# Third head pair's mask order and the start of the recurrence in a one-layer hybrid encoder kernel

## The chip, the cores and the metric

The kernel runs on one core of one Trainium2 chip, in float32. The time is device microseconds (us) of one launch; the number that is compared is the median of several executions. TensorE is called PE below, VectorE DVE, ScalarE ACT, GpSimd POOL, and SyncE, which here only issues transfers, SP.

## The reference

One layer of a two-branch block over 528 frames (16 meta tokens and 512 real ones), width 2048, and a final RMSNorm. Cut to what matters:

```python
hn = rmsnorm(h_res, norm_in_g);  P = hn @ w_in            # 2048 -> 8320 columns
Pr, Pc = P[..., :RW_COLS], P[..., RW_COLS:]
Pr = Pr + (prev(Pr) - Pr) * mu_shift                      # r, k, v, g, two low-rank inputs
# branch A, 16 heads of 64: S_t = S_{t-1} diag(w_t) - (S_{t-1} kk_t)(kk_t*a_t)^T + v_t k_t^T
#                           y_t = S_t r_t, then a norm per head, a bonus and a gate
# branch B: y_b = B * conv3(C * h) * silu(g_c)
h_res = h_res + concat(y_a, y_b) @ w_out
out = rmsnorm(h_res, norm_f_g)[:, 16:]
```

## The kernel before

**Projection.** Every matrix product in full precision is three matmuls of split operands: weights and activations are each written as a rounded high part and a low remainder (`xh`, `xl` for the activations; `hi`, `lo` of a slot `w` for the weights), and hi·xh, hi·xl and lo·xh are added up in PSUM (`steps`, matmul on L328). A column block of 128 outputs is called by what it gives: `lora`, `k`, `r`, `v`, `g` for branch A, one of each per head pair, and `C`, `h`, `B`, `gc` for branch B. The 65 blocks come one after another in the order of `plan`; this stream of matmuls is the generator `flow`. A block of 528 or 514 columns takes two PSUM banks (`ps_k_0`, `ps_k_1`) and 96 matmuls, a block of 512 takes one bank and 48. The weights come by transfers of 512 KB (`wr`, L142, three buffers), two quarters to a transfer; each quarter is cast to its high part on ACT (L134) and its low part is made on DVE or POOL (L135), in six slots `w`. A slot comes free when PE has done with the quarter in it.

**Branch A** needs a chain of small work per head pair (eight pairs). `prepare(i)` makes the operands `ar` and `bk` and multiplies them chunk by chunk (9 chunks of 64 frames) into Gram blocks; the results lie in six PSUM tiles: `g_0` in two banks of pool `pz`, `g_4` in two of pool `pi`, `g_8` in two of pool `pm`, which is the pool that the projection's blocks use as well (four banks). `masked` multiplies them by a 0/1 mask into `gt` in SBUF (L692), which frees the banks. `invert` solves two pairs' triangular blocks. `put_inverse` and the other `stash` calls write the finished operands of each pair to a buffer in device memory, `opd`. After the fourth `invert`, `recur` runs the recurrence over the chunks for all pairs at once: `load_chunk` fetches the operand tiles `ct` of a chunk, eight transfers of 320 KB, two chunks at the start and one more per step; then in each chunk three groups of small PE matmuls: `rz` from the state (L958), after ACT's `pn` (L966) the second `rz` (L973, L979), after the copies into `ct` (L988, L990) the new state's `zs` (L1005) and the output's `zy` (L1009); DVE makes the state `st` (L1020, L1021), and `norm` makes the normed output `yt`, which four transfers write to `yd` (L1051).

**What sets the order.** PE's order is written out by hand: `fill(ns)` takes matmuls out of `flow` until their estimated length (0.43 ns a column) comes to `ns`, and the numbers of `FW` say how much of the projection stands between two pieces of branch A. `FW["begin"]` is the amount between the fourth `invert` and the first `rz`; `FW["p"]`, `FW["u"]` and `FW["s"]` those inside a chunk. DVE, ACT, POOL and SP get their order from a scheduler, which places instructions by its own estimate of when they can run; `ahead()` gives an instruction a higher priority there. Each of these engines then works its own list strictly in that order.

**The end.** When all 65 blocks are through, the output projection (`M`, `P`, `Q`, L1243) runs over `m`, the split branch outputs (L1104, L1105), and a last norm goes out.

Of the kernel before, what the change touches and what calls it, by code (L numbers as in the profile page):

```python
# [41 lines left out]

FW = dict(
    evac=34, start=1062, lora=2200, gram=8000, gram_b=13500, gram2=5500, misc=2000, v=2000, vt=1000, solve=24500, solve_first=30000,
    tr=3200, lev=3000, cp=4200, out=1500, begin=19500, p=2900, u=2900, s=4800, last=3700, mix=2600,
)


# [29 lines left out]
def hymba_kernel(ctx: ExitStack, tc: tile.TileContext, xt, xtok, front, w_in, w_out, pv, lup, cst, msk, gf, out):  # L78
    nc = tc.nc
    ctx.enter_context(tc.manual_schedule(engines={mybir.EngineType.PE}))  # L80
    cp = ctx.enter_context(tc.tile_pool(name="cp", bufs=1))
# [12 lines left out]
    def col(off, i=0):  # L94
        return pvt[:, off + i : off + i + 1]
# [201 lines left out]
    with tc.issue_after(head):  # L297
        nc.vector.tensor_scalar(
            out=omm, in0=pvt[:, V_MU : V_MU + 33], scalar1=-1.0, scalar2=1.0, op0=ALU.mult, op1=ALU.add
        )  # L300
        for d, off in (
# [4 lines left out]
                out=d, in0=pvt[:, off : off + 8], scalar1=0.5, scalar2=None, op0=ALU.mult  # L306
            )
        nc.vector.tensor_scalar(
            out=hv[:, 4], in0=pvt[:, V_KA : V_KA + 8], scalar1=-0.5, scalar2=1.0, op0=ALU.mult, op1=ALU.add
# [241 lines left out]
    def fill(ns):  # L551
        while ns > 0:
            seen = len(ready)
            t = step()
            if t is None:
                return
            ns -= t
            if len(ready) > seen:
                ns += FW["evac"]
# [23 lines left out]
    def ahead():  # L583
        return tc.high_priority(offset=AHEAD)

    def c3(t):
        return t.rearrange("p (c s) -> p c s", s=CH)
# [39 lines left out]
    def prepare(i):  # L627
        p = i % 2
# [21 lines left out]
            out=bk[:, :, 1], in0=c3(k), scalar=hv[:, 2, i : i + 1], in1=c3(te), op0=ALU.mult, op1=ALU.mult  # L650
        )
        nc.gpsimd.tensor_scalar(
            out=ta, in0=ta, scalar1=hv[:, 3, i : i + 1], scalar2=hv[:, 4, i : i + 1], op0=ALU.mult, op1=ALU.add
        )
        nc.vector.scalar_tensor_tensor(
            out=ar[:, :, 0], in0=c3(k), scalar=col(V_KK, i), in1=e1[:, :, 0:CH], op0=ALU.mult, op1=ALU.mult
# [9 lines left out]
            out=ar[:, 1:NCH, 1], in0=c3(r), in1=e1[:, 1:NCH, 1 : CH + 1], op=ALU.mult  # L666
        )
        nc.vector.scalar_tensor_tensor(
            out=r, in0=r, scalar=hv[:, 5, i : i + 1], in1=ta[:, CH:LP], op0=ALU.mult, op1=ALU.mult
# [10 lines left out]
        def gram(z, c, c0):  # L680
            for h, hs, ho in heads:
                nc.tensor.matmul(  # L682
                    z[h][:, c - c0],
                    bk[hs, c, h : h + 2, :].rearrange("p a s -> p (a s)"),
                    ar[hs, c].rearrange("p a s -> p (a s)"),
                    start=True, stop=True,
                )

        def masked(z, c0, c1):
            with ahead():  # L690
                for h in range(2):
                    nc.vector.tensor_tensor(  # L692
                        out=gt[:, h, c0:c1],
                        in0=z[h],
                        in1=gmask[:, h].unsqueeze(1).to_broadcast([P, c1 - c0, P]),
                        op=ALU.mult,
                    )


        za = [pz.tile([P, 4, P], F32, tag="tz", name=f"g{i}_0_{h}") for h in range(2)]  # L700
        zc = [pi.tile([P, 4, P], F32, tag=("misc", "ser")[h], name=f"g{i}_4_{h}") for h in range(2)]
        ze = [pm.tile([P, 1, P], F32, tag="main", name=f"g{i}_8_{h}") for h in range(2)]
        for c in range(NCH):
            gram((za, zc, ze)[c // 4], c, c // 4 * 4)
        masked(za, 0, 4)
        masked(zc, 4, 8)
        masked(ze, 8, 9)
        fill(FW["gram2"] - shift + 1300 * (i == 1) + 2000 * (i == 3))

        n2 = tr(f"n2{i}")  # L710
# [59 lines left out]
        for m in (2, 4, 8):  # L770
            for b in range(16 // (2 * m)):
# [4 lines left out]
                    out=pq,  # L776
# [5 lines left out]
                    out=tq.rearrange("p (i j) -> p i j", i=m), in_=pq, op=ALU.add, axis=AX.X  # L782
                )
                nc.vector.tensor_tensor(
                    out=pq,
# [276 lines left out]
    for i in range(0, NPAIR, 2):  # L1062
        invert([prepare(i), prepare(i + 1)])
# [9 lines left out]
    mix = [pp.tile([P, 4, SEQ], F32, tag=f"R{m}", name=f"mix{m}") for m in range(4)]  # L1073
# [256 lines left out]
    for half in range(2):  # L1330
        for g in range(4):
            b, m1, m2 = U[half, "P5", g], U[half, "M1", g], U[half, "M2", g]
# [39 lines left out]
    z = {}  # L1372
# [154 lines left out]
```

## Time and profile before

| | us |
|---|---|
| median of three runs | 1000.99 (1000.61 to 1001.63) |
| the profiled execution | 999.8 |
| its span, first to last instruction | 997.9 |
| matmuls on PE | 986.4 busy, 9211 of them |
| DVE, ACT, POOL busy | 691.5, 412.7, 268.2 |
| first matmul of the recurrence | at 629.1 |
| last matmul of the recurrence | at 769.6 |
| first matmul of the output projection | at 837.2 |

The span is shorter than the execution by what lies before the first and after the last instruction. Of the lists that follow, the waits name the engine that sat idle and what ended it; a line of the timeline gives start, length, engine, line, tile written and tiles read, a count where instructions are merged, and in brackets the idle time ahead of it.

### The profile page before, as it was taken

The page shows a single profiled execution, that of the slowest core. Times are in us where ns is not written, and L with a number is a line of the kernel's source. Part 1 is how long each engine was busy: PE and PEld are TensorE (multiplying, and loading weights), DVE is VectorE, ACT ScalarE, POOL GpSimd, SP SyncE. Part 2 cuts the span into 40 slices and gives each one's busy share as a digit, 9 for nine tenths or more (in the row PEclk, how much of TensorE's full clock was granted, in tenths as well). Part 3 has the DMA queues.
Part 4 walks back from the last instruction along what each step waited for, and adds up shares of the span by engine and source line. Part 5 has one row for each costly group of instructions (what it writes and reads, how often), then busy time and mean ns, then how long its engine had stood idle before and what let it go on. Part 6 is the DMA issues. An engine that isn't in the chain of part 4 may idle for free.

```text
span 997.9 us, 22790 instructions
## 1 busy us (share of the span) xinstructions
PE 986.4 (99%) x9211; PEld 911.0 (91%) x9211; DVE 691.5 (69%) x1314; ACT 412.7 (41%) x770; POOL 268.2 (27%) x286
## 2 busy tenths in 40 slices
PE   9999999999999999999999999999999999999996
PEld 8999999999998999998999998989889898888885
DVE  7687975487765679735579735246555598999895
ACT  7554432353422534232534323233333325645553
POOL 0123323234322324222324222223242422011001
PEclk9999999999999999999999999999999999999998
DMA  9527485437683465854264854988783698698644
GB/s 337 155 70 198 112 218 150 115 105 179 149 226 108 107 178 128 221 148 118 84 180 119 224 142 125 355 259 281 219 262 94 195 260 229 212 297 218 143 102 168
DMA packets 184986, 179.48 MB, mean 180 GB/s; under 512 B 112177, under 2 KB 141617, under 8 KB 184369
## 3 DMA queue, kind: packets, MB, share of 16 engines
q1 hardware_dynamic: 182288, 169.12, 57.9%
q0 software_dynamic: 2304, 8.39, 4.9%
q8 instruction: 72, 1.18, 0.5%
q10 hardware_dynamic: 288, 0.52, 0.1%
q14 instruction: 34, 0.27, 0.1%
HBM read 139.28 MB, written 38.71 MB: 178 GB/s over the span
## 4 chain that ended last, share of the span: by engine, by line
PE 96%; DVE 1%; DMA 1%; issue 1%; POOL 0%; ACT 0%; DVEq 0%; POOLq 0%
PE ps_r L328 9%; PE ps_h L328 9%; PE ps_g L328 9%; PE ps_gc L328 9%; PE ps_B L328 9%; PE ps_v L328 9%; PE ps_C L328 8%; PE ps_k L328 8%; PE M L1243 8%; PE P L1243 4%; PE Q L1243 2%; PE g L682 2%; DMA ct<-opd 1%; PE ps_lora L328 1%; PE rz L958 1%; PE zs L1005 1%
## 5 line engine op out<-in xcount | busy, mean ns | idle before, releaser
L134 ACT CAST w<-wr 128x512 fp32r<-128x512 f32 x252 | 153.4, 619 | 281.0 <-PE ps_h L328 44.7
L135 POOL TENSOR_TENSOR w<-wr,w 128x512 fp32r<-128x512 f32 x119 | 165.8, 1395 | 371.5 <-ACT w L134 331.6
L135 DVE TENSOR_TENSOR w<-wr,w 128x512 fp32r<-128x512 f32 x133 | 99.2, 751 | 99.8 <-ACT w L134 99.6
L328 PE MATMUL ps_r<-xh,w 128*128 128x256 f32 (+1 forms) x512 | 95.2, 282 | 1.0 <-DVE gt L692 1.0
L328 PE MATMUL ps_k<-xh,w 128*128 128x256 f32 (+1 forms) x512 | 95.4, 284 | 0.0
L328 PE MATMUL ps_v<-xh,w 128*128 128x272 f32 (+1 forms) x512 | 95.4, 284 | 0.0
L328 PE MATMUL ps_h<-xh,w 128*128 128x258 f32 (+1 forms) x512 | 93.4, 282 | 0.0
L328 PE MATMUL ps_C<-xh,w 128*128 128x258 f32 (+1 forms) x512 | 93.2, 281 | 0.0
L328 PE MATMUL ps_g<-xh,w 128*128 128x258 f32 (+1 forms) x512 | 91.7, 280 | 0.0
L328 PE MATMUL ps_B<-xh,w 128*128 128x512 f32 x256 | 83.1, 394 | 0.0
L328 PEld LDWEIGHTS ps_r<-xh,w 128*128 128x128 f32 x512 | 80.2, 189 | 1.6 <-DVE gt L692 1.2
L328 PE MATMUL ps_gc<-xh,w 128*128 128x512 f32 x256 | 81.7, 393 | 0.0
L328 PEld LDWEIGHTS ps_k<-xh,w 128*128 128x128 f32 x512 | 80.3, 189 | 0.3
L328 PEld LDWEIGHTS ps_v<-xh,w 128*128 128x128 f32 x512 | 80.1, 189 | 0.3
L328 PEld LDWEIGHTS ps_C<-xh,w 128*128 128x128 f32 x512 | 79.6, 189 | 0.6
L328 PEld LDWEIGHTS ps_h<-xh,w 128*128 128x128 f32 x512 | 79.2, 189 | 0.7
L328 PEld LDWEIGHTS ps_g<-xh,w 128*128 128x128 f32 x512 | 79.2, 189 | 0.2
L328 PE MATMUL ps_k<-xl,w 128*128 128x256 f32 (+1 forms) x256 | 73.0, 285 | 0.0
L328 PE MATMUL ps_v<-xl,w 128*128 128x256 f32 (+1 forms) x256 | 72.5, 283 | 0.0
L328 PE MATMUL ps_g<-xl,w 128*128 128x256 f32 (+1 forms) x256 | 72.4, 283 | 0.0
L328 PE MATMUL ps_r<-xl,w 128*128 128x256 f32 (+1 forms) x256 | 72.1, 282 | 0.0
L328 PE MATMUL ps_C<-xl,w 128*128 128x256 f32 (+1 forms) x256 | 71.9, 281 | 0.0
(312 smaller groups left out, 2205.8 us busy)
## 6 DMA issues: line engine op xcount, KB each, us to landing
wr<-in_w_in_dram SPq DMA_DIRECT2D x126, 512.0 KB
ct<-opd SPq DMA_DIRECT2D x56, 320.0 KB
wo<-in_w_out_dram SPq DMA_DIRECT2D x21, 512.0 KB
opd<-gt SPq DMA_DIRECT2D x16, 576.0 KB
x<-in_w_out_dram POOLq DMA_DIRECT2D x16, 512.0 KB, 5.7
opd<-ar SPq DMA_DIRECT2D x8, 576.0 KB
opd<-bt SPq DMA_DIRECT2D x64, 64.0 KB
ct<-opd SPq DMA_DIRECT2D x16, 256.0 KB
```

The costliest lines, as they stand in the source:

```text
L134: nc.scalar.copy(hi, rq)
L135: low[q] = eng.tensor_tensor(out=lo, in0=rq, in1=hi.bitcast(F32), op=ALU.subtract).ins
L328: nc.tensor.matmul(ps[r], ww[:, w], xx[:, kt, a:b], start=(kt == 0 and n == 0), stop=(kt == KT - 1 and n == 2))
L682: nc.tensor.matmul(z[h][:, c - c0], bk[hs, c, h : h + 2, :].rearrange("p a s -> p (a s)"), ar[hs, c].rearrange("p a s -> p (a s)"), start= ...
L958: nc.tensor.matmul(z[e][ho if e else hs, 0, k], ct[e][hs, k, o : o + CH], uv(e, k, hs, h) if part else st[hs, 4 * e + k], start=(part == 0 ...
L1005: nc.tensor.matmul(zs[hs, j], bb[:, h], uv(e, k, everything, h), start=True, stop=True)
L1243: nc.tensor.matmul(bank[s], left(prod, jj, m, s), w, start=(jj == 0 and n == 0), stop=(jj == 7 and n == 2))
```

## The change

Two edits. The loop that masks the six Gram tiles calls `masked` for `ze` (the `g_8` tiles, in the pool shared with the projection) ahead of `za` and `zc`, for pair `i == 2` alone; and `FW["begin"]` goes from 19500 to 20300, so that `fill` takes 800 ns more of projection before `recur`.

```diff
-    tr=3200, lev=3000, cp=4200, out=1500, begin=19500, p=2900, u=2900, s=4800, last=3700, mix=2600,
+    tr=3200, lev=3000, cp=4200, out=1500, begin=20300, p=2900, u=2900, s=4800, last=3700, mix=2600,
...
-        masked(za, 0, 4)
-        masked(zc, 4, 8)
-        masked(ze, 8, 9)
+        for z, a, b in ((ze, 8, 9), (za, 0, 4), (zc, 4, 8)) if i == 2 else ((za, 0, 4), (zc, 4, 8), (ze, 8, 9)):
+            masked(z, a, b)
```

The new loop is a line shorter than the old calls, so lines behind 705 carry a number less by one in the changed kernel.

The first place is DVE's list at the masks of the third pair (`gt_2919`; `g_0`, `g_4`, `g_8` are the tiles of `za`, `zc` and `ze`, their second number the head), in the changed kernel:

```order
L135 TENSOR_TENSOR w_2858<-wr_2856,w_2858 128x512
L692 TENSOR_TENSOR gt_2919<-g_0_0_2920,cs 128x512
L692 TENSOR_TENSOR gt_2919<-g_0_1_2921,cs 128x512
L692 TENSOR_TENSOR gt_2919<-g_4_0_2922,cs 128x512
L692 TENSOR_TENSOR gt_2919<-g_8_0_2924,cs 128x128
L692 TENSOR_TENSOR gt_2919<-g_4_1_2923,cs 128x512
L692 TENSOR_TENSOR gt_2919<-g_8_1_2925,cs 128x128
L352 TENSOR_TENSOR pr_k_2969<-ps_k_0_2801,rs 128x256
```

The list before has these eight rows in the same order with the same names, and no list of any engine differs ahead of the recurrence: the scheduler put the six masks where it had put them.

The second place is PE's list at the first `rz` of the recurrence, which stands inside block `h` of group 0 (`ps_h`). Before:

```order
L328 MATMUL ps_h_0_8289<-xh,w_8110 128x256
L328 MATMUL ps_h_0_8289<-xl,w_8110 128x256
L328 MATMUL ps_h_0_8289<-xh,w_8110 128x256 x2
L328 MATMUL ps_h_0_8289<-xl,w_8110 128x256
L328 MATMUL ps_h_0_8289<-xh,w_8110 128x256 x2
L328 MATMUL ps_h_0_8289<-xl,w_8110 128x256
L958 MATMUL rz_0_8323<-ct_0_8303 64x64 x2
L958 MATMUL rz_1_8324<-ct_0_8304 64x64 x2
```

and in the changed kernel, from the last two of these rows of `ps_h_0` on:

```order
L328 MATMUL ps_h_0_8289<-xh,w_8110 128x256 x2
L328 MATMUL ps_h_0_8289<-xl,w_8110 128x256
L328 MATMUL ps_h_0_8289<-xh,w_8110 128x256 x2
L328 MATMUL ps_h_0_8289<-xl,w_8110 128x256
L328 MATMUL ps_h_0_8289<-xh,w_8110 128x256
L328 MATMUL ps_h_1_8290<-xh,w_8110 128x258
L328 MATMUL ps_h_1_8290<-xl,w_8110 128x258
L328 MATMUL ps_h_1_8290<-xh,w_8110 128x258
L957 MATMUL rz_0_8330<-ct_0_8310 64x64 x2
L957 MATMUL rz_1_8331<-ct_0_8311 64x64 x2
```

Seven matmuls of the block have moved ahead of the recurrence; the number of matmuls is the same. All later groups of the recurrence have moved likewise, by 7 or 8 matmuls in the blocks of 96 and by 4 in those of 48, which are twice as long.

The third place is ACT's list around the first cast of chunk 3 (`pn` and `ct_3` are the recurrence's, `w` the weight slots). Before:

```order
L381 ACTIVATE th_c_8903<-gc_8901 128x512
L1040 ACTIVATE yt_8878<-yc_8877 128x512
L966 ACTIVATE pn_8969<-rz_0_8935 128x256
L966 ACTIVATE pn_8969<-rz_1_8936 128x256
L134 CAST w_8909<-wr_8907 128x512
L990 COPY ct_3_8658<-rz_1_8936 64x4x64 x2
L134 CAST w_8912<-wr_8907 128x512
```

and in the changed kernel:

```order
L381 ACTIVATE th_c_8903<-gc_8901 128x512
L1039 ACTIVATE yt_8882<-yc_8881 128x512
L134 CAST w_8909<-wr_8907 128x512
L965 ACTIVATE pn_8985<-rz_0_8951 128x256
L965 ACTIVATE pn_8985<-rz_1_8952 128x256
L134 CAST w_8912<-wr_8907 128x512
L989 COPY ct_3_8662<-rz_1_8952 64x4x64 x2
```

A weight cast that stood behind the two `pn` now stands ahead of them, and the next one ahead of the copies into `ct`. The same swap with `pn` is found in chunks 4 and 5, the one with the copies in chunks 2 and 4; on DVE the making of a low part stands ahead of the state in chunks 1 and 2.

## The prediction

> **What bounds the kernel now.** I read the page first, for the engine that is never idle, then the list of PE's waits, since only those can be won back, and then the timeline at each of them.
>
> ```profile
> span 997.9 us, 22790 instructions
> PE 986.4 (99%) x9211; PEld 911.0 (91%) x9211; DVE 691.5 (69%) x1314; ACT 412.7 (41%) x770; POOL 268.2 (27%) x286
> PE 96%; DVE 1%; DMA 1%; issue 1%; POOL 0%; ACT 0%; DVEq 0%; POOLq 0%
> ```
>
> PE is busy for 986.4 of 997.9 us and the chain that ended last runs through it for 96% of the span. So the number of matmuls sets the time, and a change of order counts only where it opens or closes a gap on PE. All the gaps that the trace finds are these:
>
> ```profile
> engine line waited for: us in total, times, longest us
> PE pwarm L187 <- DVE cold L184: 1.4, 1, 1.4
> PE ps_r L328 <- DVE gt L692: 1.0, 1, 1.0
> PE rz L958 <- DMA ct<-opd: 0.5, 2, 0.3
> PE rz L979 <- issue: 0.4, 1, 0.4
> ```
>
> The first is the start of the program and stays. The second is the third pair's masks, the third the recurrence's first matmuls waiting for operands from memory, the fourth a stop in chunk 3 for which the profile shows no cause. The last three come to 1.9 us, which is the most that any new order of this work could give back between the first and last matmul: 0.19% of 1000.99. What a measurement of this kernel can tell from no change is about 0.2%, or 2.0 us.
>
> **The masks.** The wait of 1.0 us is seen at the third pair, on PE and on DVE:
>
> ```profile
> 217.80 0.29 PE L328 MATMUL ps_k<-xh,w 128*128 128x272 f32 x1
> 219.04 0.38 PE L328 MATMUL ps_r<-xh,w 128*128 128x256 f32 x1 [0.96 <-DVE gt L692]
> ...
> 216.92 2.87 DVE L692 TENSOR_TENSOR gt<-g,cs 128x512 f32<-128x512 f32 x6
> ```
>
> Block `r` of the fourth pair needs the bank that `g_8_0` holds, and DVE frees it as the fourth of six masks, at about 219.0; had that small mask come first, at 216.92, the bank would have been free before PE asked for it at 218.08, and 0.96 us would be gained. But the calls are written in a new order and the list that DVE works is the same as before, row for row: the scheduler had already drawn `g_8_0` ahead of `g_4_1`, and the new order of calls does not move it. DVE's list, PE's list and the instructions ahead of both are the same, so PE waits here as before. Term: 0. Its bounds are 0 and −0.96, and I take 0 because the list is what the engine runs.
>
> **The later start.** Seven matmuls of block `h` now stand ahead of the first `rz`. What it met before:
>
> ```profile
> 629.13 0.58 PE L958 MATMUL rz<-ct 64*64 64x64 f32 x24
> 629.87 0.33 PE L958 MATMUL rz<-ct 64*64 64x64 f32 x4 [0.17 <-DMA ct<-opd]
> 630.55 0.33 PE L958 MATMUL rz<-ct 64*64 64x64 f32 x4 [0.35 <-DMA ct<-opd]
> ...
> 630.88 3.37 PE ps_h L328 x27
> 677.45 1.09 PE rz L958 x64
> 678.54 3.39 PE ps_C L328 x27
> 681.93 0.62 PE rz L973 x32
> ```
>
> The 32 matmuls go pair by pair of heads; the seventh pair's operands held PE for 0.17 us and the eighth's for 0.35, together 0.52. One matmul of block `h` takes 3.37/27 = 0.125 us, so seven put the first `rz` off by 0.87 us, from 629.13 to 630.00. An undisturbed `rz` matmul takes 1.09/64 = 0.017 us, so the four that wait for the eighth pair are reached 28 × 0.017 = 0.48 us later, at 630.48. These operands were there at 630.55: the transfers are ordered on SP ahead of anything that the change moves, and nothing in their waits depends on the new place of the recurrence, so they land when they landed. A wait of 0.07 us is left, and 0.52 − 0.07 = 0.45 us is won. Its bounds are −0.52 (they land 0.07 us earlier) and 0 (they land later by as much as PE comes later).
>
> **What the later start pushes.** The seven matmuls are not new work: they no longer follow `rz`, so PE's sum is the same, and every group of the recurrence keeps its distance from the next, `fill` being unchanged between them. Three things move against each other.
>
> First, the weight casts that now stand ahead of `pn` on ACT in chunks 3, 4 and 5. In chunk 3 ACT did this:
>
> ```profile
> 676.68 0.63 ACT L1040 ACTIVATE yt<-yc 128x512 f32<-128x512 f32 x1
> 678.58 0.66 ACT L966 ACTIVATE pn<-rz 128x256 f32<-128x256 f32 x2 [1.27 <-PE rz L958]
> 679.56 0.62 ACT L134 CAST w<-wr 128x512 fp32r<-128x512 f32 x1 [0.32 <-ACT pn L966]
> ...
> 668.49 2.03 SPq L142 DMA_DIRECT2D wr<-in_w_in_dram  x2
> 671.91 4.08 SPq L937 DMA_DIRECT2D ct<-opd  x8
> ```
>
> The cast waits for a slot, which PE frees with the last matmul of a quarter, the 24th of block `C`. Before, `rz` stood behind the 18th; now it stands behind the 26th, so the slot is free two matmuls, 0.25 us, before `rz` begins. The cast takes 0.62 us and `rz` 1.09 us, so ACT is free again 0.72 us before `rz` ends and `pn` may start: 0. If the cast should come late, `pn` has room: it ended at 679.24 and the L973 that reads it began at 681.93, 2.69 us later. The same reckoning holds where a cast stands ahead of the copies in chunks 2 and 4 and a low part ahead of the state in chunks 1 and 2: the slot is freed before the small matmuls whose results the next row waits for, and these take longer (1.09 us for L973 with L979 in the sum of their rows, 2 us for L1005 with L1009) than the cast, or the cast and the low part (0.62 and 0.69 us).
>
> Second, the transfers. The weights of that cast are asked for at 668.49 and needed some 9.7 us later, at about 678.2; the nearest row for how long a burst takes is the first chunk's operands, for which the chain of waits has the two pieces
>
> ```profile
> 619.47 5.72 DMA ct<-opd
> 625.21 5.30 DMA ct<-opd
> ```
>
> which is 11.1 us for 16 transfers, twice what stands in the queue behind these weights. One or two transfers ahead of the burst should land well within 9.7 us. Term: 0.
>
> Third, the end. The recurrence ends 0.87 us later among the blocks of the projection, and what depends on it ends so much later:
>
> ```profile
> 825.47 1.02 DVE L1105 TENSOR_TENSOR m<-mix,m 128x256 fp32r<-128x256 f32 x2
> 837.22 8.33 PE L1243 MATMUL M<-w,m 128*128 128x512 f32 x36
> ```
>
> The last branch outputs of branch A are ready at 826.49, and PE reads them from 837.22 on: 10.7 us of cover against 0.87. Term: 0, and if that cover were gone the cost would be the 0.87.
>
> The fourth gap, 0.4 us at L979 in chunk 3, has no cause in the profile. It may be gone (−0.42) or come twice (+0.42); I take 0.
>
> **The sum** for the profiled execution: 0 − 0.45 + 0 + 0 + 0 = −0.45 us, a span of 997.45 in place of 997.9. That execution took 999.8 us, 1.2 below the median, so I take the difference over to the median: 1000.99 − 0.45 = 1000.54, which I give as 1000.5.
>
> **The rivals.**
>
> *The masks act after all.* Then 0.96 us is won besides: 1000.99 − 0.45 − 0.96 = 999.6. For it speaks that the wait is real and the edit is aimed at it; against it, that DVE's list does not change. Chance 0.06.
>
> *Nothing comes back.* The first chunk's operands land later by as much as PE does, or the time won at 630 is lost at another wait of the same size (the stop at L979 coming twice costs 0.42): 1001.0. For it speaks that the share of the transfer engines is over 0.9 at that time,
>
> ```profile
> 615.00:630.00 15.00, 14.83 (x141) 14.26 (x139) 5.50 (x9) 3.74 (x6) 3.50 (x3) 1.00 0.77 257
> 630.00:646.00 16.00, 15.65 (x230) 14.49 (x230) 3.84 (x8) 4.45 (x9) 3.39 (x4) 1.00 0.92 334
> 646.00:662.00 16.00, 16.00 (x242) 12.97 (x241) 8.41 (x13) 5.21 (x12) 3.73 (x4) 1.00 0.95 321
> 662.00:678.00 16.00, 16.00 (x239) 13.38 (x235) 8.46 (x13) 5.58 (x12) 5.72 (x5) 1.00 0.75 242
> ```
>
> (the last columns are the granted clock, the share of the transfer engines and GB/s), so that a landing can move by some tenths of a us; against it, that no transfer ahead of these has moved. Chance 0.16.
>
> *Slower: ACT is held by a weight.* In chunks 3, 4 and 5 a cast now stands ahead of `pn`, on an engine that works in order. It decides from the point where the weights land so late that `pn` misses L973: in chunk 3 at 681.93 − 0.66 − 0.62 = 680.65, or 12.2 us after they were asked for. Each us behind that is a us on PE in each of three chunks; at 13.2 us it is 3 × 1.0 = 3.0, and the time 1004.0. For it speaks the order of the list and that the transfer engines are at least three quarters busy in the windows of the first chunks (0.75 to 0.95 in the rows above); against it, the 2.69 us of room and the 11.1 us that a burst of double size took. The Trainium skill bears on this rival: its page "TensorE: Matmul & The Clock Gate", in the section on the array's architectural detail, says that ScalarE and VectorE are strict first-in first-out queues and that only TensorE can draw weight loads forward. By that rule the swapped cast does hold `pn` whenever its slot or its weights are late, and the edit would cost 3.0 us; the trace agrees in so far as ACT's `pn` and casts of the rows above run in the order of the list, but shows no cast that was late. Chance 0.12.
>
> **How the numbers follow.** The forecast has 0.66, with 1000.5. Its own range: one run of this kernel stands up to 0.9 us from the middle of the four times shown (999.8 to 1001.63 is 1.83), and the unexplained stop adds 0.42 on either side. Low: 1000.54 − 0.42 − 0.9 = 999.2, which takes in the masks' 999.6. High: the rival without any gain, 1000.99 + 0.42 + 0.9 = 1002.3. Outside lie the slower rival and the tails. Faster by over 0.2% is under 998.99: even all three gaps closed, 1000.99 − 1.9 = 999.1, would not do it, so only a run of luck does, 0.06. Slower by over 0.2%, over 1002.99, is the slower rival and a little beside: 0.13. Within: 0.81.
>
> **What would show it.** Right: in the changed kernel's list of PE's waits the row of L958 is down to 0.1 us or gone, the row of `ps_r` for the masks still has 1.0, DVE's masks of the third pair still run in the order 512, 512, 512, 128, 512, 128, and PE is busy for the same 986.4 us. Wrong: the row of L958 as before or larger (the landing moved); the masks' row gone (the order did change); a new row of L973 waiting for `pn`, or of L1005 waiting for a copy into `ct` (the swapped casts hold ACT); or a new wait for `w` or `m` between 770 and 840 us, which would mean that I read the cover at the end wrongly.

## The result, and the profile after

| | before | after |
|---|---|---|
| median of 22 runs each, taken in turn (us) | 1001.55 (1000.08 to 1002.52) | 999.88 (998.83 to 1000.77) |
| after : before | | 0.9984 [0.9978, 0.999] |
| the profiled execution, its span | 999.8, 997.9 | 999.89, 998.0 |

The change takes 1.6 us off (1.0 to 2.2 by the interval). It is less than the 0.2% named in the prediction, but 22 runs of each kernel tell it from nothing. The two profiled executions do not show it in their spans: the one of before was the fastest seen of that kernel (its 22 timed runs begin at 1000.08), the one of after stands at its median. So they are compared by stretches between the same two instructions, not by their ends.

The head of the page of the changed kernel (busy time by engine, and the chain of waits by engine):

```profile
span 998.0 us, 22792 instructions
PE 986.7 (99%) x9211; PEld 910.8 (91%) x9211; DVE 689.2 (69%) x1314; ACT 412.2 (41%) x770; POOL 271.6 (27%) x286
PE 95%; DMA 2%; DVE 1%; issue 1%; POOL 0%; ACT 0%; DVEq 0%; SPq 0%; POOLq 0%
```

and its list of PE's waits:

```profile
engine line waited for: us in total, times, longest us
PE pwarm L187 <- DVE cold L184: 1.4, 1, 1.4
PE ps_r L328 <- DVE gt L692: 1.0, 1, 1.0
PE rz L957 <- DMA ct<-opd: 0.3, 1, 0.3
PE ps_lora L328 <- DVE xl L208: 0.2, 1, 0.2
PE z L870 <- issue: 0.2, 1, 0.2
```

The 9211 matmuls take the same time as before. The masks' wait is still 1.0 us. The wait for the first operands is down from 0.5 us in two to 0.3 in one, and the stop at the third group of chunk 3 (L979, now L978) is not in the list. Two stops of 0.2 us are new, in the first block and at the first `invert` (`z`); both stand ahead of anything that the change moves.

The timeline of PE in the changed kernel, at the landmarks that the stretches are measured by (the first row is the start of the fourth `invert`; then chunk 0's first group and the block behind it, chunk 3's third group and the block behind it, and the output projection):

```profile
590.63 1.16 PE L854 MATMUL t<-xn,gt 64*64 64x64 f32 x64
...
630.97 0.81 PE L957 MATMUL rz<-ct 64*64 64x64 f32 x28
632.11 0.33 PE L957 MATMUL rz<-ct 64*64 64x64 f32 x4 [0.33 <-DMA ct<-opd]
632.37 0.39 PE L328 MATMUL ps_h<-xh,w 128*128 128x258 f32 x1
...
684.00 0.65 PE L978 MATMUL rz<-st,ct 64*64 64x64 f32 x32
684.58 0.51 PE L328 MATMUL ps_C<-xh,w 128*128 128x256 f32 x2
...
837.30 8.34 PE L1242 MATMUL M<-w,m 128*128 128x512 f32 x36
```

The same view of the kernel before, the rows that the prediction did not show:

```profile
589.60 1.16 PE L855 MATMUL t<-xn,gt 64*64 64x64 f32 x64
...
630.81 0.51 PE L328 MATMUL ps_h<-xh,w 128*128 128x256 f32 x2
...
682.38 0.63 PE L979 MATMUL rz<-st,ct 64*64 64x64 f32 x29
683.43 0.33 PE L979 MATMUL rz<-st,ct 64*64 64x64 f32 x3 [0.42 <-issue]
683.68 0.39 PE L328 MATMUL ps_C<-xh,w 128*128 128x258 f32 x1
```

From the fourth `invert` to the output projection it was 837.22 − 589.60 = 247.62 us and is now 837.30 − 590.63 = 246.67: 0.95 less in this pair of executions. The changed kernel had reached the `invert` 1.03 us later, so the spans come out alike. Within the stretch, two places became shorter:

- **Chunk 0's first group**, from its first matmul to the first of the block behind it: 630.81 − 629.13 = 1.68 us before, 632.37 − 630.97 = 1.40 after.
- **Chunk 3's third group**, likewise: 683.68 − 682.38 = 1.30 before, 684.58 − 684.00 = 0.58 after.

These two differences, 0.28 and 0.72, make 1.00, all of the 0.95 to within 0.05. The same stretches in every kernel that ran are the yardstick of the experiments:

| kernel | begin | first group | chunk 3, third group | fourth `invert` to `M` | third pair's Gram to the fourth's |
|---|---|---|---|---|---|
| before | 19500 | 1.68 | 1.30 | 247.62 | 48.92 |
| e1 masks' calls alone | 19500 | 1.95 | 1.48 | 248.06 | 48.95 |
| e6 small Gram block first | 19500 | 2.09 | 1.40 | 248.11 | 47.73 |
| e5 first operands in two parts | 19500 | 0.73 | 1.08 | 246.44 | 48.95 |
| e7 eight matmuls more at the start | 19500 | 0.95 | 0.58 | 246.16 | 48.92 |
| e3 earlier start | 18700 | 2.92 | 0.57 | 248.23 | 48.93 |
| after | 20300 | 1.40 | 0.58 | 246.67 | 48.92 |
| e2 later start alone | 20300 | 1.24 | 0.58 | 246.52 | 48.95 |
| e4 later still | 21100 | 0.62 | 0.58 | 245.87 | 48.92 |
| e8 later still | 22700 | 0.62 | 0.58 | 245.82 | 48.88 |
| e9 e6's edit and e4's start | 21100 | 0.63 | 0.58 | 245.87 | 47.73 |
| e10 e6's edit and e8's start | 22700 | 0.62 | 0.58 | 245.81 | 47.73 |

Before, e1 and e6 have the same work in the same order on PE from the fourth `invert` on, and so have after and e2. Their means are 247.93 and 246.60: the change takes 1.33 us out of this stretch, against 1.6 timed.

### The profile page after: what moved, and what is told of

Read it like the earlier page. It is cut to its first block, busy times and chain, and to the rows that moved or that the text cites. A ratio compares the mean times of both kernels' runs of the same rounds, so it can differ in the third digit from the quotient of the medians.

```text
span 998.0 us, 22792 instructions
## 1 busy us (share of the span) xinstructions
PE 986.7 (99%) x9211; PEld 910.8 (91%) x9211; DVE 689.2 (69%) x1314; ACT 412.2 (41%) x770; POOL 271.6 (27%) x286
## 4 chain that ended last, share of the span: by engine, by line
PE 95%; DMA 2%; DVE 1%; issue 1%; POOL 0%; ACT 0%; DVEq 0%; SPq 0%; POOLq 0%
PE ps_g L328 9%; PE ps_r L328 9%; PE ps_h L328 9%; PE ps_gc L328 9%; PE ps_B L328 9%; PE ps_v L328 9%; PE ps_C L328 8%; PE ps_k L328 8%; PE M L1242 8%; PE P L1242 4%; PE Q L1242 2%; PE g L682 2%; DMA ct<-opd 1%; PE ps_lora L328 1%; PE rz L957 1%; PE zs L1004 1%
## 5 line engine op out<-in xcount | busy, mean ns | idle before, releaser
L135 POOL TENSOR_TENSOR w<-wr,w 128x512 fp32r<-128x512 f32 x119 | 168.2, 1415 | 365.2 <-ACT w L134 326.7
L328 PE MATMUL ps_h<-xl,w 128*128 128x256 f32 (+1 forms) x256 | 72.5, 283 | 0.0
```

The costliest lines, as they stand in the source:

```text
L135: low[q] = eng.tensor_tensor(out=lo, in0=rq, in1=hi.bitcast(F32), op=ALU.subtract).ins
L328: nc.tensor.matmul(ps[r], ww[:, w], xx[:, kt, a:b], start=(kt == 0 and n == 0), stop=(kt == KT - 1 and n == 2))
```

## The experiments

The leading theory, A in the expectations, was that the later start does all of it, through two places: the first group, whose loss is larger than its listed waits, and the stop at L979. Against it stood that the masks' calls matter (B), and, later, that gains do not add up since a PE that comes early meets the next wait (D), and that every further step of the start brings as much again (E). C in the expectations puts the gain down to the order of the lists in later chunks and not to the first wait. All ratios are to runs of the kernel before on the same chip, differences in us are the ratio times 1000.

**e1, the masks' calls alone.**

```diff
-        masked(za, 0, 4)
-        masked(zc, 4, 8)
-        masked(ze, 8, 9)
+        for z, a, b in ((ze, 8, 9), (za, 0, 4), (zc, 4, 8)) if i == 2 else ((za, 0, 4), (zc, 4, 8), (ze, 8, 9)):
+            masked(z, a, b)
```

> Only the calls of the masks in the new order, FW['begin'] at 19500 as before. Theory A (the whole change is the later start of the recurrence; the scheduler puts the masks where they were): 0.0 us against before, PE's wait of 1.0 us for the masks is still there. Rival B (the new order of calls acts on the chip): -1.0 us, and that wait is gone.

Measured: 1001.07 against 1001.25, ratio 0.9998 [0.9989, 1.0007]. Of its list of PE's waits:

```profile
PE ps_r L328 <- DVE gt L692: 0.9, 1, 0.9
PE rz L957 <- DMA ct<-opd: 0.7, 2, 0.3
PE rz L978 <- issue: 0.6, 1, 0.6
```

All three waits of the kernel before are there. The interval, −1.1 to +0.7 us, takes in B's −1.0 only at its edge, and the wait that B would remove is unchanged: this half of the change does nothing that the runs show, and B falls.

**e2, the later start alone.**

```diff
-    tr=3200, lev=3000, cp=4200, out=1500, begin=19500, p=2900, u=2900, s=4800, last=3700, mix=2600,
+    tr=3200, lev=3000, cp=4200, out=1500, begin=20300, p=2900, u=2900, s=4800, last=3700, mix=2600,
```

> Only FW['begin'] at 20300, masks called as before. Theory A: all of the change's gain, -1.6 us against before, split into about -0.9 at the recurrence's first matmuls (the operands of the eighth pair came 0.94 us late, the shift is 0.87) and about -0.7 from the stop at L979 in chunk 3 that the profile of the changed kernel no longer has. Rival B: about -0.6, the rest being the masks'.

Measured: 999.94, ratio 0.9989 [0.998, 0.9998], or −1.1 us (−2.0 to −0.2). In the table its two groups, 1.24 and 0.58, stand with those of after, and its long stretch, 246.52, with that of after, 246.67. This half is the whole change, as far as the intervals can tell.

**e3 and e4, the start one step earlier and one later.** `begin=18700` and `begin=21100` in the same place, the masks' calls as before.

> FW['begin'] at 18700: the recurrence starts 800 ns of projection earlier than before. Theory A (PE waits for the first chunk's operands, whose landing does not depend on PE): +0.9 us against before, and the group of first matmuls takes 2.6 us from start to end where it took 1.75. Rival C (the gain comes from the other order of the lists in later chunks, not from the first wait): within 0.3 us of before.

> FW['begin'] at 21100: 1600 ns of projection later than before. Theory A: the first wait is gone, -1.2 us at the first matmuls against before, in all -1.2 to -1.9 depending on whether the stop at L979 is there. Rival C: no rule for it, but no more than 0.3 us apart from the kernel with 20300 only by chance; it would show as a first group of unchanged length.

Measured: earlier, 1002.61, ratio 1.0011 [1.0002, 1.002], or +1.1 us (0.2 to 2.0); later, 998.96, ratio 0.998 [0.9971, 0.9989], or −2.0 us (−2.9 to −1.1). PE's timeline of e3 at the first group:

```profile
628.45 0.46 PE L958 MATMUL rz<-ct 64*64 64x64 f32 x16
629.24 0.33 PE L958 MATMUL rz<-ct 64*64 64x64 f32 x4 [0.33 <-DMA ct<-opd]
629.79 0.33 PE L958 MATMUL rz<-ct 64*64 64x64 f32 x4 [0.22 <-DMA ct<-opd]
630.46 0.33 PE L958 MATMUL rz<-ct 64*64 64x64 f32 x4 [0.33 <-DMA ct<-opd]
631.11 0.33 PE L958 MATMUL rz<-ct 64*64 64x64 f32 x4 [0.32 <-DMA ct<-opd]
631.37 0.39 PE L328 MATMUL ps_h<-xh,w 128*128 128x256 f32 x1
```

and of e4:

```profile
630.50 0.69 PE L958 MATMUL rz<-ct 64*64 64x64 f32 x32
631.12 0.39 PE L328 MATMUL ps_h<-xl,w 128*128 128x258 f32 x1
```

The start decides how many of the eight pairs' operands PE has to wait for: four at 18700, two at 19500 (before, e1 and e6), one at 20300, none at 21100. So the first group changes with every step, against C. The group takes 2.92 us at the one end and 0.62 at the other, with the same 32 matmuls. The four listed waits of e3 come to 1.2 us, and the group is 2.92 − 0.62 = 2.30 longer: each stop costs about 0.3 us more than the idle time that is written at it. The earlier start has no stop at L979 (0.57), so over the long stretch it loses less than in its first group: that stretch is 0.30 above that of before's order.

**e5, the first operands in two parts.** If the first group's wait is a matter of the landing alone, it can be taken away without moving the start: the columns that the first `rz` reads are fetched first, for all pairs, and the others behind them.

```diff
-        for i in pairs:
-            nc.sync.dma_start(ops[c, i % 2][:, i // 2, a:b], spot(i, 0, P, c, 1, 1, a, b - a))
+        for a, b in ((O_G, O_B), (O_B, OPW)) if c == 0 else ((a, b),):
+            for i in pairs:
+                nc.sync.dma_start(ops[c, i % 2][:, i // 2, a:b], spot(i, 0, P, c, 1, 1, a, b - a))
```

> FW['begin'] at 19500 and PE's order as before; the operands of chunk 0 come in two parts, first the 384 columns that the first matmuls read (192 KB a transfer), then the 128 columns that zs reads later. Theory A (late operands): with a quarter less to bring, the eighth pair's operands land some 1.5 to 2 us earlier, the first group runs in 0.55 us in place of 1.75, and the time is -1.2 us against before; the stop at L979 may stay. Rival C (other lists, not the first wait): within 0.3 us of before.

Measured: 1000.29 against 1001.16, ratio 0.9993 [0.9984, 1.0002], or −0.7 us (−1.6 to +0.2): the timed runs alone do not tell the theories apart. In its profile the group is one piece, and the stop at the third group of chunk 3 (here L980) is still there:

```profile
629.98 0.80 PE L959 MATMUL rz<-ct 64*64 64x64 f32 x32
630.71 0.50 PE L328 MATMUL ps_h<-xh,w 128*128 128x256 f32 x2
...
682.29 0.63 PE L980 MATMUL rz<-st,ct 64*64 64x64 f32 x28
683.11 0.33 PE L980 MATMUL rz<-st,ct 64*64 64x64 f32 x4 [0.19 <-issue]
683.37 0.39 PE L328 MATMUL ps_C<-xh,w 128*128 128x258 f32 x1
```

The long stretch is 247.93 − 246.44 = 1.49 us shorter than the mean of before's order; 0.31 of this is its shorter stop (1.08 against a mean of 1.39). The wait for the first operands was therefore worth about 1.2 us, where the list of waits has 0.5 for before and 0.7 for e1. PE's order is that of before here, so this part of the gain does not need another order of PE's list: C falls for the first wait. And the stop at the third group does not depend on that wait, since it is there without it.

**e6, the masks in earnest.** PE makes the small block, chunk 8's, first, so that its masks can come first on DVE.

```diff
-        for c in range(NCH):
+        for c in (8, *range(8)) if i == 2 else range(NCH):
             gram((za, zc, ze)[c // 4], c, c // 4 * 4)
-        masked(za, 0, 4)
-        masked(zc, 4, 8)
-        masked(ze, 8, 9)
+        for z, s, t in ((ze, 8, 9), (za, 0, 4), (zc, 4, 8)) if i == 2 else ((za, 0, 4), (zc, 4, 8), (ze, 8, 9)):
+            masked(z, s, t)
```

> FW['begin'] at 19500; for the third pair the Gram block of chunk 8 is multiplied first on PE and its masks are called first, so that DVE's list has g_8_0 and g_8_1 ahead of the other four. Theory A (the edit of the masks would gain its wait, had it reached DVE's list): PE's wait of 1.0 us for the masks is gone, -1.0 us against before. Rival D (the wait only moves on, to the other banks or to the next block): 0.0 us.

Measured: 999.7, ratio 0.9985 [0.9976, 0.9993], or −1.5 us (−2.4 to −0.7). DVE's and PE's timeline of e6 at the masks:

```profile
218.34 2.87 DVE L692 TENSOR_TENSOR gt<-g,cs 128x128 f32<-128x128 f32 x6
...
219.23 0.29 PE L328 MATMUL ps_k<-xh,w 128*128 128x272 f32 x1
219.35 0.28 PE L328 MATMUL ps_r<-xh,w 128*128 128x256 f32 x1
```

The merged row of the six masks now begins with a 128x128 one, and `ps_r` follows `ps_k` at once. From the third pair's Gram blocks to the fourth's it is 47.73 us in place of 48.92: 1.2 won, for a wait listed as 0.96. The order of the calls alone does not bring this about (e1); together with the order in which PE makes the blocks it does. PE's order alone was not run.

**e7, eight matmuls more at the start.** The stop at L979 has no releaser in the profile. In all four profiles that have PE's list of the recurrence as before, and as many matmuls ahead of it (before, e1, e5, e6), it stands in the same place, behind the 28th or 29th matmul of that group; in none of those with another start. To see whether it hangs on the place in PE's list, eight 32-column matmuls were added at the program's start, and nothing else was moved; the trace has them as 16.

```diff
+    for _ in range(8):
+        nc.tensor.matmul(pwarm[:, 0:32], cold[:, 0:P], cold[:, 0:32], start=True, stop=True)
```

> Before, with eight matmuls of 32 columns more at PE's start (their result is not used), which shift every later PE instruction by eight matmuls' worth of instructions and nothing in the order. Theory F (the stop behind the 29th matmul of L979 in chunk 3 lies at a fixed count of PE's instructions): the stop moves by eight matmuls, behind the 21st, or is gone where it was; -0.7 us if gone, less up to 0.5 us for the eight at the start. Rival G (the stop belongs to what happens around it): it stays behind the 29th, and the time is that of before plus 0 to 0.5 us.

Measured: 1001.13, ratio 1.0005 [0.9994, 1.0016]. The timeline of PE at that group (here L981):

```profile
683.63 0.65 PE L981 MATMUL rz<-st,ct 64*64 64x64 f32 x32
684.21 0.39 PE L330 MATMUL ps_C<-xh,w 128*128 128x258 f32 x1
```

The stop is gone, and did not turn up earlier in the group either, where theory F would have it if it stood at a fixed count of PE's instructions. The timed runs show no gain. In the profile the added matmuls cost more than the 0.5 us that was allowed for them: the projection's first matmul starts at 7.21 us, against 4.60 in before and 4.63 in after, and the first of `ps_v` still comes at 55.19, against 53.23 and 53.80. Those 1.4 to 2.0 us are about the 247.93 − 246.16 = 1.77 by which the long stretch is shorter. Its first group had no listed wait in this execution: these operands had landed early. That the whole program ran later does not explain the missing stop, since e1 ran later too (its fourth `invert` at 591.00, before's at 589.60, e7's at 591.59) and has the longest stop of all. So the work of the recurrence alone does not bring the stop about, and a shift of PE's list goes with its absence, as far as one profile of each kernel can tell. That the shift is the cause is not shown, and what PE stops for is open.

**e8, how far it goes.** `begin=22700`, the masks' calls as before.

> FW['begin'] at 22700, 3200 ns of projection later than before. Theory A: the first wait is gone as it was at 21100, so nothing more is won: -2.3 us against before, as at 21100, within 0.5. Rival E (a later start is better in itself, about -1.3 us for each 800 ns as from 18700 to 21100): -4.9 us.

Measured: 999.76, ratio 0.9984 [0.9976, 0.9993], or −1.6 us (−2.4 to −0.7), where A had −2.3 and E −4.9. The long stretch is 245.82, e4's is 245.87. Beyond 21100 these two places have nothing left to win, and nothing is lost yet either. E, more with every step, falls.

**e9 and e10, both together.** e6's edit with `begin=21100` and with `begin=22700`.

> FW['begin'] at 21100 and, for the third pair, the Gram block of chunk 8 multiplied first with its masks called first. Theory A (two separate gaps on PE, each closed): the sum of the two alone, -1.2 us of the masks and -2.0 of the first wait and the stop at L979, -3.2 us against before, and none of the three in the list of PE's waits. Rival D (a gap closed early only meets the operands of the recurrence earlier): -2.0 us, with a wait for ct back, since PE comes 1.2 us sooner to transfers that do not come sooner.

> The same with FW['begin'] at 22700. Theory A: -3.2 us as at 21100, within 0.5. Rival D: nearer to -3.2 than the kernel with 21100, which would be at -2.0.

Measured, against 1001.5: 998.78, ratio 0.9979 [0.9971, 0.9988], and 998.05, ratio 0.9969 [0.9959, 0.998], or −3.1 us (−4.1 to −2.0). The list of PE's waits of e10, whole:

```profile
engine line waited for: us in total, times, longest us
PE pwarm L187 <- DVE cold L184: 1.4, 1, 1.4
PE z L870 <- issue: 0.2, 1, 0.2
```

By the table both should win 1.2 us at the masks and 247.93 − 245.8 = 2.1 behind the `invert`, 3.3 in all. e10's interval takes that in; e9's −2.1 (−2.9 to −1.2) falls short of it and is the number that D had, but the wait for operands by which D explained it was not in its profile (first group 0.63). Nor do the transfers stay where they were when PE comes sooner: in e6 too they start 619.69 − 589.82 = 29.87 us behind the `invert`, as in before. e9's profile instead has two waits of `M` for DVE's `o` at the output projection, 0.7 us together; whether its timed runs had them is not known, and why it falls short stays open. The two intervals overlap, so whether 22700 is better than 21100 in company with e6's edit is not settled. By its ratio e10 is the fastest version here.

## Why the prediction was right or wrong

It said 1000.5, 0.45 us below the median it was given, with no difference as the likeliest outcome by 0.2%. The kernel gained 1.6, three and a half times as much. The sign and the part that gains were right; one term was put at nothing that was 0.8, and another came near its size for a reason that was incomplete. That the new median lies between the 999.2 and 1002.3 of the prediction is due to the width of that range, most of which is the spread of single runs.

**The masks, 0: right.** The wait stayed at 1.0, DVE's merged row of the six masks in the changed kernel (at 217.99) still begins with a 128x512 one, and e1 shows the edit alone at 0.9998. DVE's list was the right thing to read; the rival "the masks act after all" falls.

**The later start, −0.45: near in size, but by two errors that cancel.** By the table the first group fell from a mean of (1.68 + 1.95 + 2.09)/3 = 1.91 to (1.40 + 1.24)/2 = 1.32 us: −0.59. The working could win back no more than the listed idle time, 0.52 us. Yet this group lost 1.68 − 0.62 = 1.06 us in that execution, since around each stop PE loses more than the idle time listed. What ends the group is the landing of the last operands, before and after; as long as that holds, starting later wins as much as the start moves, whatever waits are listed. The start moved by 40.34 − 39.53 = 0.81 us against the `invert`, a little less than the 0.87 that was reckoned from a row of the chain. Against this, "so they land when they landed" was too firm. The chain of waits of the changed kernel shows the transfers:

```profile
620.50 6.31 DMA ct<-opd
626.81 0.02 issue
626.83 5.23 DMA ct<-opd
632.06 0.04 issue
632.11 0.33 PE rz L957 x4
```

Their start stands at a fixed distance behind the `invert`: 620.50 − 590.63 = 29.87 us, and 619.47 − 589.60 = 29.87 before. But from there to the waiting `rz` it took 632.11 − 620.50 = 11.61 us now and 630.55 − 619.47 = 11.08 before. By the same view it was 11.35 in e1, 11.48 in e6, 11.45 in e2 and 11.40 in e3, so the one execution that the prediction rests on had the earliest landing of these six. On the means (11.30 in before's order, 11.53 in after's) the landing came 0.23 later, and 0.81 − 0.23 = 0.58 is what is expected of the rows, beside the 0.59 found.

The prediction read these two pieces as a burst of 16 transfers. They are two transfers, one behind the other: in the trace before, SP issues seven of chunk 0's eight from 619.47 on, and the eighth alone at 625.21, 0.02 us after the first has landed; of the 16, the last is issued at 630.52, when the eighth has landed. (Chunk 0's are of 256 KB each, not 320.) So what PE waits for is the eighth, and in these six executions its own 5.23 to 5.30 us hardly change: the first transfer, with 5.72 to 6.31, is what moves the landing.

**The stop at L979, 0 with bounds of 0.42 to either side: this is the term that failed.** It was there in every profile of before's order and in none of the others, and it was worth more than its row. From the group's start to the block behind it:

| | listed idle | start to block | above 0.58 |
|---|---|---|---|
| e5 | 0.19 | 1.08 | 0.50 |
| before | 0.42 | 1.30 | 0.72 |
| e6 | 0.51 | 1.40 | 0.82 |
| e1 | 0.59 | 1.48 | 0.90 |

The loss is the listed idle plus 0.30 or 0.31 each time. The mean of before, e1 and e6 is 0.81, and all of it came back. With −0.59 this makes −1.40, where the long stretch has −1.33 and the timed runs −1.6 (−2.2 to −1.0). "It may be gone (−0.42) or come twice (+0.42)" treated a row without a cause as chance. The prediction had itself counted that every later group moves in PE's list, and did not weigh that such a stop may come and go with that; the cause of the stop stays open, so it could hardly have been sure of it. And since the bound was the listed idle time, even its good end was 0.4 short of 0.81.

The remark that the last three gaps together can give back 1.9 at most fell with it. e10 has none of them left and gains 3.1 (2.0 to 4.1); by the table the three were worth 1.2 (e6), 1.3 and 0.8, together 3.3.

**The swapped casts, 0: right.** ACT's timeline in chunk 3 of the changed kernel:

```profile
678.95 0.62 ACT L134 CAST w<-wr 128x512 fp32r<-128x512 f32 x1 [0.89 <-PE ps_C L328]
680.23 0.66 ACT L965 ACTIVATE pn<-rz 128x256 f32<-128x256 f32 x2 [0.66 <-PE rz L957]
```

The cast ended at 679.57, 0.66 us before `pn` could start (0.72 was expected), and the list of waits has no row for `pn`, for a copy into `ct` or for `w`. No run had a cast that came late, so the rule of the Trainium skill that the prediction set beside this rival (strict order on ScalarE, in "TensorE: Matmul & The Clock Gate", the section on the array's architectural detail) was not put to the test. Against this rival the prediction set a burst of double size that took 11.1 us; since that row was two transfers in succession, it was no measure of a burst. The weights in question came in time: in the trace of the changed kernel their two transfers, asked for at 669.25 and 670.80, landed at 674.29 and 675.54 (the last update of each one's semaphore), before the cast at 678.95, which had waited for PE.

**The transfers and the end, 0 and 0: right.** There is no new wait for `w` or `m`; even at 22700, where the first `rz` stands 42.9 us behind the fourth `invert` in place of 39.5, the list of e10 has none.

**Taking the difference over to the median** was right and needed: set against the profile of before, with its span of 997.9, the change would have seemed worth nothing.

## What to carry to other kernels

Where a dependency lands at a fixed time, the gain of starting its reader later is the time of the work put ahead of it, up to the whole lateness of the group; read that from the group's start to the first instruction behind it, compared with an undisturbed one, since the idle times listed at the stops are only part of it. Ask also which transfer lands last, and what it was issued behind. An edit to the order of calls changes nothing where a scheduler draws up the list: look at what it may draw first, here the order in which PE makes the blocks. Compare two profiles by stretches between the same instructions, not by their spans, when the effect is smaller than the difference from one execution to the next.

## What the runs showed of the hardware

A stop of PE in a run of 64x64 matmuls cost some 0.3 us more than its listed idle time: 0.30 or 0.31 for four stops of 0.19 to 0.59 us at one place (table above). For the four stops of e3 it is (2.30 − 1.2)/4 = 0.28. The Trainium skill's page "Perfetto Trace Analysis", in its section on the tensor engine's instructions (MATMUL, LD_WEIGHTS), says that the ends that the profile gives for a matmul are estimated and not observed; the rows here agree in that the idle time, which is counted from such an end, is short of the loss between two starts.

A stop that the profile gives to nothing stood behind the 28th or 29th matmul of one group in four kernels with the same list there, at 0.19 to 0.59 us, and was gone in all eight with a shifted list, the one with eight small matmuls at the start among them. Another such stop comes and goes with the list unchanged: the one at `z` (L870, L871), 0.2 to 0.5 us long, is in six of the eleven profiles whose list is the same up to there (e1, e2, e6, e8, e10 and after). So one profile with such a stop, or without it, does not settle what the kernel does each time. The transfers of the first chunk, with their start fixed against the `invert`, took 11.08 to 11.61 us in six executions; in e7 PE was past the group at 632.07, 10.6 us behind that start (591.59 + 29.87). A transfer of 256 KB among them took 5.2 to 6.3 us (the first and the eighth of the chunk, in the chains of these six).
